# A decoder layer on one core: transposes handed out tile by tile, three jobs side by side at each stage entry, the last job by token tiles, and another beginning

## The chip, the core and the metric

The kernel runs on one core of one Trainium2 chip. The metric is the device time of one execution in microseconds; the median of several executions is taken. A difference is called faster or slower in the text below where it is over 0.2%.

## What is computed

One decoder layer for 256 tokens of width 2048, in float32, cut to its skeleton (16 heads of 128, inner width 5632 of the feed-forward nets; with 256 tokens the block-sparse attention is a plain causal one):

```
x = x + 0.5 * (silu(n(x) @ Wg1) * (n(x) @ Wu1)) @ Wd1        # FFN 1, n = RMSNorm with gain
z = n(x) @ W_in                                              # q, k, v, B, C, xt, two gates
y_a = attention(q, k, v) @ W_attn_out                        # causal, ALiBi
y_c = (B * causal_conv3(C * xt)) @ W_conv_out
x = x + (sigmoid(g_a) * y_a + sigmoid(g_c) * y_c) @ W_out
x = x + 0.5 * (silu(n(x) @ Wg2) * (n(x) @ Wu2)) @ Wd2        # FFN 2
out = n(x)
```

## The kernel before, in words

Weights are streamed once from memory, 467 MB in all, in chunks that are normally 128x1024 (512 KB). Each chunk passes three stages: a DMA issued by SP (`load`, L567) into one of five buffers; a cast on ACT to the matmul type, which gives the high part `hi` (L580); a subtraction on DVE, which gives the low part `lo` (L581). The weight is then used as hi + lo, and the activations are split in the same way (`split_col`: ACT L98 or L101, DVE L99 or L102). `hi` and `lo` have four buffers each. `parts` in the main loop cuts chunk n+4 into hi and lo while TensorE works on chunk n, and issues the load of chunk n+7, so at most a few chunks are ahead. ACT, DVE, PE and SP each work through their own queue in the order in which the program was written.

There are two kinds of jobs. A plain job (`job`, L183 and L184) multiplies one 128-column strip of weights with all 16 column tiles of the activations `xn`; it takes two chunks and 16 pairs of matmuls (512 and 256 columns), and its result is turned into the next activation by a few ACT and DVE operations, the job's `post`. A wide job (`wide_job`, L222 to L224) makes 512 columns of the residual for both token tiles: eight chunks, twelve 512-column matmuls for each chunk. Four wide jobs (nb = 0 to 3) close FFN 1, the mixer and FFN 2. Behind each of them `residual` adds to `x` (DVE L246 or L248), squares it for the next norm (ACT L132), and `turn` transposes the 512 new columns on TensorE (8 transposes, L236) and splits them into `xn` (L101, L102). A stage entry (seam) is the stretch from these four wide jobs to the next stage's first jobs: f1 to mixer and mixer to FFN 2.

Posts wait in a list, `pending`. After each chunk of a job one entry of it is written into the program (`flush(1)`). A step without chunks, such as the preload of the Sqrt table ahead of wide job nb = 1, writes all of them at once (`flush()`). The norm of a stage needs the sum over the four wide jobs. It is held back: `norm_steps` puts the first half behind the first plain job and the row of scales (two matmuls, L162) behind the second.

At the beginning `first_block` runs four plain jobs side by side in groups of four column tiles, with chunks of 256 KB, while x arrives transposed as `xin` (xT, SP). The sum of squares for the first norm is made from `xin` by 16 squares on ACT (L118, L121), 14 additions on DVE (L122) and matmuls with `ones` (L144), ahead of the block's last four pairs. The token-major `x` is loaded later, in four pieces, by SP. At the end the final norm scales the 2048 columns of both token tiles (DVE L644, ACT L646), and SP writes them out in four pieces of 512 KB. `load_gain` loads the final gain into one buffer for each last wide job (L262, SP).

## Time and profile before

| | |
|---|---|
| median of 3 runs | 2536.82 us (2535.48 to 2537.56) |
| the profiled execution, its own time | 2535.27 us |
| its span, first to last instruction | 2533.5 us |
| PE busy | 2485.4 us, 98% |
| PE weight loads | 2148.9 us, 85% |
| DVE busy | 1557.4 us, 61% |
| ACT busy | 1175.2 us, 46% |
| mean granted TensorE clock | 0.992 |
| read from memory | 466.68 MB, 185 GB/s over the span |

Busy time is that of instructions at work. A PE that waits or runs at the lower of its two clocks (1.2 of 2.4 GHz, a granted clock of 0.50 in a row) loses time in a way that the share does not show alike: the wait is idle, the slow matmuls count as busy. Times in rows count from the start of the span.

### The profile page before, as it was taken

The page shows a single profiled execution, that of the slowest core. Times are in us where ns is not written, and L with a number is a line of the kernel's source. Part 1 is how long each engine was busy: PE and PEld are TensorE (multiplying, and loading weights), DVE is VectorE, ACT ScalarE, POOL GpSimd, SP SyncE. Part 2 cuts the span into 40 slices and gives each one's busy share as a digit, 9 for nine tenths or more (in the row PEclk, how much of TensorE's full clock was granted, in tenths as well). Part 3 has the DMA queues.
Part 4 walks back from the last instruction along what each step waited for, and adds up shares of the span by engine and source line. Part 5 has one row for each costly group of instructions (what it writes and reads, how often), then busy time and mean ns, then how long its engine had stood idle before and what let it go on. Part 6 is the DMA issues. An engine that isn't in the chain of part 4 may idle for free.

```text
span 2533.5 us, 34394 instructions
## 1 busy us (share of the span) xinstructions
PE 2485.4 (98%) x13380; PEld 2148.9 (85%) x13380; DVE 1557.4 (61%) x2123; ACT 1175.2 (46%) x1685; POOL 1.9 (0%) x10
## 2 busy tenths in 40 slices
PE   8999999999999999999999999999999999999998
PEld 7888888888778888888888888887888888888886
DVE  6765665566546777655556666664566566556664
ACT  5544444344444444444444454444444444444443
POOL 0000000000000000000000000000000000000000
PEclk9999999999999999999999999999999999999999
DMA  7665556655555555555555545565556655665563
GB/s 242 204 194 192 190 186 197 192 191 185 174 151 181 191 190 184 192 192 190 189 168 180 170 167 191 190 184 146 172 189 192 190 191 192 191 192 191 191 198 143
DMA packets 131715, 471.02 MB, mean 186 GB/s; under 512 B 14560, under 2 KB 14688, under 8 KB 131552
## 3 DMA queue, kind: packets, MB, share of 16 engines
q1 hardware_dynamic: 131552, 468.84, 57.3%
q8 instruction: 104, 1.70, 0.3%
q14 instruction: 59, 0.48, 0.1%
HBM read 466.68 MB, written 2.10 MB: 185 GB/s over the span
## 4 chain that ended last, share of the span: by engine, by line
PE 96%; DVE 2%; ACT 1%; DMA 1%; issue 0%; SPq 0%; ACTq 0%; DVEq 0%
PE ps L183 46%; PE ps L184 23%; PE pv L222 7%; PE pv L224 7%; PE pv L223 7%; PE pv L447 1%; PE pv L445 1%; PE pv L446 1%; ACT hi L580 1%; DVE lo L581 1%; DVE xn L102 1%; DMA w<-in_wg 0%; ACT pv L132 0%; PE psV L502 0%; PE psS L468 0%
## 5 line engine op out<-in xcount | busy, mean ns | idle before, releaser
L183 PE MATMUL ps<-xn,hi 128*128 128x512 f32 x4544 | 1586.9, 393 | 0.0
L581 DVE TENSOR_TENSOR lo<-w,hi 128x1024 fp32r<-128x1024 f32 (+1 forms) x892 | 1076.1, 1211 | 810.8 <-ACT hi L580 809.9
L184 PE MATMUL ps<-xn,lo 128*128 128x256 f32 x4544 | 1271.6, 280 | 0.0
L580 ACT CAST hi<-w 128x1024 fp32r<-128x1024 f32 (+1 forms) x892 | 919.2, 1035 | 691.9 <-PE pv L224 272.2
L183 PEld LDWEIGHTS ps<-xn,hi 128*128 128x128 f32 x4544 | 854.9, 188 | 188.0
L184 PEld LDWEIGHTS ps<-xn,lo 128*128 128x128 f32 x4544 | 854.9, 188 | 0.7
L222 PE MATMUL pv<-hi,ring 128*128 128x512 f32 x832 | 327.1, 393 | 0.0
L223 PE MATMUL pv<-lo,ring 128*128 128x512 f32 x832 | 326.1, 392 | 0.0
L224 PE MATMUL pv<-hi,ring 128*128 128x512 f32 x832 | 326.0, 392 | 0.0
L224 PEld LDWEIGHTS pv<-hi,ring 128*128 128x128 f32 x832 | 157.6, 189 | 33.1
L223 PEld LDWEIGHTS pv<-lo,ring 128*128 128x128 f32 x832 | 157.8, 190 | 32.7
L222 PEld LDWEIGHTS pv<-hi,ring 128*128 128x128 f32 x832 | 157.8, 190 | 32.8
L197 DVE TENSOR_TENSOR t<-ps,c 128x256 f32<-128x256 f32 x320 | 134.0, 419 | 23.0 <-ACT c L195 23.0
L195 ACT COPY c<-ps 128x256 f32<-128x256 f32 x320 | 116.8, 365 | 54.4 <-PE ps L184 54.4
L98 ACT CAST ring<-hh 128x256 fp32r<-128x256 f32 x88 | 35.8, 406 | 201.1 <-DVE hh L321 201.1
L314 ACT ACTIVATE silu<-t 128x256 f32<-128x256 f32 x88 | 36.8, 418 | 163.1 <-DVE t L312 163.1
L183 PE MATMUL ps<-at,hi 128*128 128x512 f32 x256 | 89.5, 392 | 0.0
L183 PE MATMUL ps<-ring,hi 128*128 128x512 f32 x256 | 89.4, 392 | 0.0
L184 PE MATMUL ps<-ring,lo 128*128 128x256 f32 x256 | 71.6, 280 | 0.0
L184 PE MATMUL ps<-at,lo 128*128 128x256 f32 x256 | 71.6, 280 | 0.0
L99 DVE TENSOR_TENSOR ring<-hh,ring 128x256 fp32r<-128x256 f32 x88 | 37.5, 427 | 41.6 <-ACT ring L98 41.6
L183 PEld LDWEIGHTS ps<-ring,hi 128*128 128x128 f32 x256 | 48.1, 188 | 10.6
(102 smaller groups left out, 1013.8 us busy)
## 6 DMA issues: line engine op xcount, KB each, us to landing
w<-in_win SPq DMA_DIRECT2D x222, 512.0 KB, 4.1
w<-in_wd SPq DMA_DIRECT2D x176, 512.0 KB, 4.1
w<-in_wu SPq DMA_DIRECT2D x172, 512.0 KB, 3.9
w<-in_wg SPq DMA_DIRECT2D x170, 512.0 KB, 3.7
w<-in_wco SPq DMA_DIRECT2D x32, 512.0 KB, 3.6
w<-in_wv SPq DMA_DIRECT2D x32, 512.0 KB, 4.2
w<-in_wao SPq DMA_DIRECT2D x32, 512.0 KB, 3.9
w<-in_wo SPq DMA_DIRECT2D x32, 512.0 KB, 3.6
```

What stands on the lines that cost most here:

```text
L98: nc.scalar.copy(dst[:, 0:T], src)
L99: nc.vector.tensor_sub(dst[:, T:2 * T], src, f32(dst[:, 0:T]))
L183: nc.tensor.matmul(ps, hi[:, j * P:(j + 1) * P], r, start=(k == 0), stop=False)
L184: nc.tensor.matmul(ps[:, 0:T], lo[:, j * P:(j + 1) * P], r[:, 0:T], start=False, stop=(k == n - 1))
L195: nc.scalar.copy(c, ps[:, T:2 * T])
L197: nc.vector.tensor_add(t, ps[:, 0:T], c)
L222: nc.tensor.matmul(pv[i], xh, hi[:, cols], start=(k == 0), stop=False)
L223: nc.tensor.matmul(pv[i], xh, lo[:, cols], start=False, stop=False)
L224: nc.tensor.matmul(pv[i], xl, hi[:, cols], start=False, stop=(k == n - 1))
L314: nc.scalar.activation(s, g, AF.Silu)
L580: nc.scalar.copy(hi, w)
L581: nc.vector.tensor_sub(lo, w, f32(hi))
```

## The change

- `turn` works on one column tile (two transposes) where it worked on four, and `residual` returns the addition, an empty entry and four such turns, so that `flush(1)` hands them out behind six chunks of the next job.
- The first three jobs of the mixer and of FFN 2 run side by side (`side_block`) in groups of four column tiles, in twelve chunks of 256 KB; the norm's columns stand behind the sixth chunk, the row of scales behind the ninth. The four jobs at the beginning use the same function.
- The first norm is made from the token-major x (`row_square_in`, four squares for each token tile on ACT), which `fetch` now loads in the middle of the first block. The row of scales stands behind the fifth job, and the posts of the block are held back till then.
- x and xT are loaded by DMAs that ACT issues, the weights by SP. Six matmuls on zeros (f32, 256 columns) are put ahead of everything on TensorE.
- The last wide job is done as two jobs, one for each token tile, each with all eight weight chunks; behind the first one `finish(0)` scales token tile 0 and writes it out in three pieces, behind the second one `finish(1)` does tile 1 in four.

```diff
-X_LOAD = 24
+GK = 4
+WARM = 6
...
-    def add_square(tag, m):
...
+    def row_square_in(i):
+
+        if "f1" not in ssq:
+            ssq["f1"] = work.tile([P, 2, NB], F32, name="ssq", tag="ssq", bufs=2)
+        for nb in range(NB):
+            nc.scalar.activation(at[:, i, :], x[:, i, nb * NW:(nb + 1) * NW], AF.Square,
+                                 accum_out=ssq["f1"][:, i, nb:nb + 1])
...
+    def norm_cols(tag, i0=0, i1=2):
...
+        nc.vector.reduce_sum(s, ssq[tag][:, i0:i1, :], axis=AX.X)
...
-    def norm_steps(tag):
...
+    def rows(tag):
+        ps = norm_row(tag)
+        R[tag] = work.tile([P, T], F32, name="R", tag="R", bufs=1)
+        nc.vector.tensor_copy(R[tag], ps[:, 0:T])
...
-    def wide_job(chunks, src, post):
+    def wide_job(chunks, src, post, tiles=(0, 1)):
...
+            pv = {i: psum_big("pv") for i in tiles}
...
-                    for i in range(2):
+                    for i in tiles:
...
-    def turn(nb, gain):
-
-        for half, tag in ((0, "psT"), (1, "psV")):
-            ps = patt.tile([P, 4 * P], F32, name=tag, tag=tag)
-            for c in range(2):
-                m = nb * 4 + half * 2 + c
-                for i in range(2):
-                    nc.tensor.transpose(ps[:, c * T + i * P:c * T + (i + 1) * P], x[:, i, m * P:(m + 1) * P], ident)
-                split_col(xn[:, m, :], ps[:, c * T:(c + 1) * T], vec(gain, m))
+        return Step(chunks, pe, [lambda q=q: q(held[0]) for q in post], shift=0)
+
+    def turn(m, gain):
+
+        tag = ("psT", "psV")[m % 2]
+        ps = patt.tile([P, 4 * P], F32, name=tag, tag=tag)
+        for i in range(2):
+            nc.tensor.transpose(ps[:, i * P:(i + 1) * P], x[:, i, m * P:(m + 1) * P], ident)
+        split_col(xn[:, m, :], ps[:, 0:T], vec(gain, m))
 
...
                 if tag == "fin":
                     nc.vector.tensor_mul(yout[:, i, cols], x[:, i, cols], grow[nb])
+                    if nb == NB - 1:
+                        finish(i)
         if tag is None or tag == "fin":
             return [add]
-        return [add, lambda pv: turn(nb, gain)]
+        return [add, lambda _: None] + [lambda _, m=m: turn(m, gain) for m in range(4 * nb, 4 * nb + 4)]
+
+    def finish(i):
+
+        norm_cols("fin", i, i + 1)
+        r = rcol["fin"]
+        cuts = (0, 6, 11, 16) if i == 0 else (0, 4, 8, 12, 16)
+        for q, (a, b) in enumerate(zip(cuts, cuts[1:])):
+            cols = slice(a * P, b * P)
+            if q % 2 == 0:
+                nc.vector.tensor_scalar(yout[:, i, cols], yout[:, i, cols], r, None, op0=ALU.mult)
+            else:
+                nc.scalar.activation(yout[:, i, cols], yout[:, i, cols], AF.Copy, scale=r)
+            nc.sync.dma_start(out[:, i, cols], yout[:, i, cols])
 
...
-    def first_block(block, norms):
...
+    def side_block(block, rhs, hooks):
+
+        chunks = [(w[:, k * P:(k + GK) * P], GK) for k in range(0, ND, GK) for w, _ in block]
...
-                if b == 0 and k0 + GK < ND:
-                    prepare(k0 + GK, k0 + 2 * GK)
-                if b == 2:
-                    for k in range(k0, k0 + GK):
-                        add_square("f1", k)
-                if k0 + GK == ND and b == 2:
-                    norms[0].pe(None)
+                for h in hooks.get(n, ()):
+                    h()
                 yield
-            norms[1].pe(None)
-
-        return Step(chunks, pe, [lambda p=b[2], n=n: p(ps[n]) for n, b in enumerate(block)])
+
+        return Step(chunks, pe, [lambda p=b[1], n=n: p(ps[n]) for n, b in enumerate(block)])
+
+    def seam_hooks(tag):
+        return {5: [lambda: norm_cols(tag)], 8: [lambda: rows(tag)]}
 
...
+            for which, w, post in (("g", wg, post_g), ("u", wu, post_u)):
+                if len(block) < (4 if first else 3):
+                    block.append((w[t], post))
+                    if first and len(block) == 4:
+                        hooks = {n: [lambda k=n + 4: prepare(k, k + 4)] for n in (0, 4, 8)}
+                        hooks[1] = [lambda: fetch(0)]
+                        hooks[5] = [lambda: fetch(1)]
+                        hooks[12] = [lambda: row_square_in(0)]
+                        steps.append(Step([], lambda _: None, hold=True))
+                        steps.append(side_block(block, rhs, hooks))
+                    elif not first and len(block) == 3:
+                        steps.append(side_block(block, rhs, seam_hooks(tag)))
+                    continue
+                late = {}
+                if first and (which, t) == ("g", 2):
+                    late = {0: lambda: (row_square_in(1), norm_cols(tag)), 1: lambda: (rows(tag), release())}
+                steps.append(job((tag, which, t), pieces(w, t), rhs, post, late))
 
...
+                split_last = last and next_tag == "fin" and nb == NB - 1
+                for tiles in ((0,), (1,)) if split_last else ((0, 1),):
+                    steps.append(wide_job(wide(wd, nb, k0, k1), lambda k, k0=k0: ring((k0 + k) % RING),
+                                          residual(nb, 0.5, next_tag if last else None, gain_next), tiles))
...
+            if len(block) < 3:
+                block.append((win[part * ND + c], post))
+                if len(block) == 3:
+                    steps.append(side_block(block, rhs, seam_hooks("mix")))
+                return
...
-            q = len(raw) - X_LOAD
-            if q in (0, 2, 4, 6):
-                cols = slice(q * T, (q + 2) * T)
-                nc.sync.dma_start(x[:, :, cols], xt[:, :, cols])
...
+    def fetch(i):
+        nc.scalar.dma_start(x[:, i, :], xt[:, i, :])
+
     open_ring()
-    nc.scalar.preload_act_table(AF.Sqrt)
-    nc.sync.dma_start(xin[:, 0:2, :], xT[:, 0:2, :])
+    nc.scalar.dma_start(xin[:, 0:2, :], xT[:, 0:2, :])
     nc.sync.dma_start(cs[:, 0:NCST], cst)
     load(1)
-    nc.sync.dma_start(xin[:, 2:4, :], xT[:, 2:4, :])
-    load(2)
-    for i in range(1, 4):
-        nc.sync.dma_start(xin[:, 4 * i:4 * i + 4, :], xT[:, 4 * i:4 * i + 4, :])
-        load(min(LOAD_AHEAD, 2 + 2 * i))
-    nc.vector.memset(ones, 1.0)
+    nc.scalar.dma_start(xin[:, 2:4, :], xT[:, 2:4, :])
+    load(3)
+    nc.scalar.dma_start(xin[:, 4:8, :], xT[:, 4:8, :])
+    load(5)
+    nc.scalar.preload_act_table(AF.Sqrt)
+    nc.vector.memset(x[:, 0, 0:T], 0.0)
+    warm = patt.tile([P, 4 * P], F32, name="psS", tag="psS")
+    for _ in range(WARM):
+        nc.tensor.matmul(warm[:, 0:T], x[:, 0, 0:P], x[:, 0, 0:T], start=True, stop=True)
     make_identity(nc, ident)
...
+    nc.scalar.dma_start(xin[:, 8:12, :], xT[:, 8:12, :])
+    nc.scalar.dma_start(xin[:, 12:16, :], xT[:, 12:16, :])
...
-    norm_cols("fin")
-    r = rcol["fin"]
-    for q in range(2):
...
```

What this does to the order, at three places. First TensorE where the first wide job of the mixer's seam ends (pv: the wide jobs' accumulators, psT and psV: the two transpose buffers). Before:

```order
L224 MATMUL pv1_5980<-hi_6064,ring_91 128x512
L236 MATMUL psT_6139<-ident_85,x_79 128x128 x4
L236 MATMUL psV_6148<-ident_85,x_79 128x128 x4
L222 MATMUL pv0_6158<-hi_6082,ring_91 128x512
L223 MATMUL pv0_6158<-lo_6083,ring_91 128x512
```

and now, at the same place:

```order
L211 MATMUL pv_5943<-hi_6027,ring_90 128x512
L221 MATMUL psT_6102<-ident_84,x_79 128x128 x2
L221 MATMUL psV_6107<-ident_84,x_79 128x128 x2
L221 MATMUL psT_6112<-ident_84,x_79 128x128 x2
L221 MATMUL psV_6117<-ident_84,x_79 128x128 x2
L209 MATMUL pv_6123<-hi_6045,ring_90 128x512
```

The eight transposes of nb = 0 still stand in one clump ahead of the next wide job, in four pairs instead of two fours. Those of nb = 1, 2 and 3 stand apart, two behind each of four chunks of the following job.

Second DVE in the last wide job, where the split of tile 1's fourth chunk is over:

```order
L233 SCALAR_TENSOR_TENSOR x_79<-pv_22184,x_79 128x512
L238 TENSOR_TENSOR sacc_82<-x_79,grow_22182 128x512
L136 TENSOR_REDUCE rc_22303<-ssq_21873 128x1
L137 TENSOR_SCALAR rc_22303<-rc_22303 128x1
L139 RECIPROCAL rc_22303<-rc_22303 128x1
L140 TENSOR_TENSOR rc_22303<-rc_22303 128x1
L141 TENSOR_TENSOR rc_22303<-rc_22303 128x1
L142 TENSOR_SCALAR rc_22303<-rc_22303 128x1
L143 TENSOR_TENSOR rc_22303<-rc_22303 128x1
L253 TENSOR_SCALAR sacc_82<-sacc_82,rc_22303 128x768
L253 TENSOR_SCALAR sacc_82<-sacc_82,rc_22303 128x640
L579 TENSOR_TENSOR lo_22321<-w_22263,hi_22320 128x1024
```

All of tile 0's residual, norm and scaling now stands between the splits of two weight chunks, the last row being that of tile 1's fifth chunk; before, all this stood behind the last split.

Third SP at the same place (w_22318 is the last weight chunk of the program):

```order
L569 DMA w_22275<-in_wd2 128x1024
L569 DMA w_22288<-in_wd2 128x1024
L256 DMA out_y<-sacc_82 128x768
L256 DMA out_y<-sacc_82 128x640 x2
L569 DMA w_22318<-in_wd2 128x1024
L256 DMA out_y<-sacc_82 128x512 x4
```

The load of the last chunk has moved behind the three writes of tile 0; before, no write stood ahead of a load.

## Rows read from the trace of the kernel before

**Rows 1.** The profile's page: busy time of each engine

```profile
PE 2485.4 (98%) x13380; PEld 2148.9 (85%) x13380; DVE 1557.4 (61%) x2123; ACT 1175.2 (46%) x1685; POOL 1.9 (0%) x10
```

**Rows 2.** Who waited for whom, PE: total us, times, longest us

```profile
PE psT L236 <- DVE xn L102: 13.9, 8, 3.0
PE psV L236 <- DVE xn L102: 9.7, 8, 1.3
```

**Rows 3.** Windows: stretch, us, busy PE, PEld, DVE, ACT, POOL, clock, DMA share, GB/s

```profile
492.60:659.00 166.40, 166.40 (x961) 146.52 (x960) 108.32 (x148) 79.71 (x118) 0.00 (x0) 1.00 0.58 189
1250.00:1540.00 290.00, 290.00 (x1609) 253.14 (x1608) 180.21 (x280) 147.80 (x243) 0.00 (x0) 1.00 0.52 173
...
659.00:781.12 122.12, 109.77 (x487) 89.67 (x485) 59.41 (x74) 52.10 (x75) 0.00 (x0) 0.94 0.52 156
1682.48:1804.88 122.40, 110.06 (x486) 89.74 (x485) 59.83 (x74) 52.09 (x75) 0.00 (x0) 0.94 0.52 156
2180.89:2267.96 87.07, 87.07 (x386) 72.08 (x385) 44.81 (x43) 34.31 (x34) 0.00 (x0) 1.00 0.64 195
...
2521.43:2533.50 12.07, 0.16 (x1) 0.00 (x0) 4.76 (x13) 3.83 (x7) 0.00 (x0) 0.66 0.42 174
685.59:689.00 3.41, 3.41 (x10) 2.74 (x10) 0.66 (x2) 2.80 (x3) 0.00 (x0) 0.50 0.00 0
...
2527.00:2532.00 5.00, 0.00 (x0) 0.00 (x0) 0.00 (x0) 0.57 (x1) 0.00 (x0) 0.50 1.02 419
```

**Rows 4.** Timeline behind the mixer seam's first wide job: start, us, instruction, idle before

```profile
680.56 0.39 PE L224 MATMUL pv<-hi,ring 128*128 128x512 f32 x1
...
681.84 0.33 PE L236 MATMUL psT<-ident,x 128*128 128x128 f32 x1 [0.27 <-DVE x L248]
...
682.46 0.45 ACT L101 ACTIVATE xn<-psT,cs 128x256 fp32r<-128x256 f32 x1
682.94 0.48 DVE L102 SCALAR_TENSOR_TENSOR xn<-psT,cs,xn 128x256 fp32r<-128x256 f32 x1 [1.16 <-ACT xn L101]
683.48 0.44 PE L236 MATMUL psT<-ident,x 128*128 128x128 f32 x2 [1.32 <-DVE xn L102]
...
685.59 0.76 PE L222 MATMUL pv<-hi,ring 128*128 128x512 f32 x1
```

**Rows 5.** Timeline, PE, begin and end of the first block

```profile
5.60 0.79 PE L285 MATMUL ps<-xn,hi 128*128 128x512 f32 x1 [5.60 <-ACT hi L580]
...
35.56 1.87 PE L144 MATMUL psS<-ones,acc 128*128 128x1 f32 x8 [4.04 <-DVE acc L122]
...
40.60 0.48 PE L183 MATMUL ps<-xn,hi 128*128 128x512 f32 x1
```

**Rows 6.** Groups by form, 5 to 34 us: count, busy us, mean ns, idle before

```profile
L581 DVE TENSOR_TENSOR lo<-w,hi 128x512 fp32r<-128x512 f32 x16 | 10.5, 688 | 1.2 <-ACT hi L580 1.2
L580 ACT CAST hi<-w 128x512 fp32r<-128x512 f32 x16 | 9.6, 614 | 1.7 <-DMA w<-in_wg 1.1 <-PE ps L285 0.4
```

**Rows 7.** Groups by form, last wide job and tail (2499.66 us to the end)

```profile
L581 DVE TENSOR_TENSOR lo<-w,hi 128x1024 fp32r<-128x1024 f32 x5 | 6.0, 1223 | 5.0 <-ACT hi L580 4.8
...
L580 ACT CAST hi<-w 128x1024 fp32r<-128x1024 f32 x5 | 5.2, 1049 | 4.6 <-DMA w<-in_wd 2.7 <-PE pv L224 1.9
...
L248 DVE SCALAR_TENSOR_TENSOR x<-pv,x 128x512 f32<-128x512 f32 x4 | 2.7, 686 | 7.8 <-PE pv L224 7.8
L132 ACT ACTIVATE pv<-x 128x512 f32<-128x512 f32 x4 | 2.4, 603 | 12.9 <-DVE x L248 12.9
```

**Rows 8.** Timelines of SP, ACT and DVE, last wide job and tail

```profile
2504.87 0.33 SPq L262 DMA_DIRECT2D grow<-in_gf  x1
...
2509.47 1.05 ACT L580 CAST hi<-w 128x1024 fp32r<-128x1024 f32 x1 [2.71 <-DMA w<-in_wd]
...
2523.76 0.16 DVE L147 TENSOR_REDUCE rc<-ssq 128x2 f32<-128x8 f32 x1
...
2525.38 2.19 ACT L646 ACTIVATE sacc<-sacc,rc 128x1024 f32<-128x1024 f32 x2 [1.02 <-DVE rc L155]
```

More of the change, by code (lines that the diff above doesn't have):

```diff
@@ L83, in macaron_kernel @@
     cs = const.tile([P, NCST], F32, name="cs")
-    ones = const.tile([P, 4 * LINE], F32, name="ones")[:, 0:1]
     ident = const.tile([P, P], F32, name="ident")
     dist = const.tile([P, 3 * P], F32, name="dist")
-    work.tile([P, LINE], F32, name="padw", tag="padw", bufs=1)
+    work.tile([P, LINE + 120], F32, name="padw", tag="padw", bufs=1)
     def vec(off, i):
@@ L133, in row_square @@
                              accum_out=ssq[tag][:, i, nb:nb + 1])
-    def norm_cols(tag):
-        r = work.tile([P, 8], F32, name="rc", tag="rc", bufs=2)
-        v, s, y = r[:, 0:2], r[:, 2:4], r[:, 4:6]
-        if tag in acc:
-            ps = patt.tile([P, 4 * P], F32, name="psS", tag="psS")
-            a = acc.pop(tag)
-            for i in range(2):
-                for j, t in enumerate(a):
-                    nc.tensor.matmul(ps[:, i:i + 1], t[:, i * P:(i + 1) * P], ones, start=(j == 0), stop=(j == 1))
-            total = ps[:, 0:2]
-        else:
-            nc.vector.reduce_sum(s, ssq.pop(tag), axis=AX.X)
-            total = s
-        nc.vector.tensor_scalar(v, total, 1.0 / D, EPS, op0=ALU.mult, op1=ALU.add)
+    def row_square_in(i):
[5 more added lines that the diff above has]
+    def norm_cols(tag, i0=0, i1=2):
+        n = i1 - i0
+        r = work.tile([P, 8], F32, name="rc", tag="rc", bufs=3)
+        v, s, y = r[:, 0:n], r[:, 2:2 + n], r[:, 4:4 + n]
+        nc.vector.reduce_sum(s, ssq[tag][:, i0:i1, :], axis=AX.X)
+        nc.vector.tensor_scalar(v, s, 1.0 / D, EPS, op0=ALU.mult, op1=ALU.add)
         nc.scalar.activation(s, v, AF.Sqrt)
@@ L164, in norm_row, with job @@
         return ps
-    def norm_steps(tag):
-        def row(_):
-            ps = norm_row(tag)
-            R[tag] = work.tile([P, T], F32, name="R", tag="R", bufs=1)
-            nc.vector.tensor_copy(R[tag], ps[:, 0:T])
-        return (Step([], lambda _: norm_cols(tag), hold=True), Step([], row, hold=False))
-    def job(name, chunks, rhs, post):
+    def rows(tag):
+        ps = norm_row(tag)
+        R[tag] = work.tile([P, T], F32, name="R", tag="R", bufs=1)
+        nc.vector.tensor_copy(R[tag], ps[:, 0:T])
+    def job(name, chunks, rhs, post, hooks={}):
         n = sum(c[1] for c in chunks)
@@ L179, in pe @@
             k = 0
-            for hi, lo, nk in parts:
+            for n_done, (hi, lo, nk) in enumerate(parts):
                 for j in range(nk):
@@ L270, in switch @@
         steps.append(Step([], pe))
-    def first_block(block, norms):
-        GK = 4
-        chunks = [(w[t][:, k * P:(k + GK) * P], GK) for k in range(0, ND, GK) for w, t, _ in block]
+    def side_block(block, rhs, hooks):
+        chunks = [(w[:, k * P:(k + GK) * P], GK) for k in range(0, ND, GK) for w, _ in block]
         ps = []
@@ L324, in gu @@
             rhs = lambda k: xn[:, k, :]
-            if first and t < 2:
-                block.append((wg, t, post_g))
-                block.append((wu, t, post_u))
-                return
-            steps.append(job((tag, "g", t), pieces(wg, t, CK if t else CK // 2), rhs, post_g))
-            if t == 0:
-                steps.append(norms[0])
-            steps.append(job((tag, "u", t), pieces(wu, t), rhs, post_u))
-            if t == 0:
-                steps.append(norms[1])
+            for which, w, post in (("g", wg, post_g), ("u", wu, post_u)):
[15 more added lines that the diff above has]
+                steps.append(job((tag, which, t), pieces(w, t), rhs, post, late))
         t = 0
@@ L340, in ffn @@
                 t += 1
-                if first and t == 2:
-                    steps.append(first_block(block, norms))
             last = r == len(ROUNDS) - 1
@@ L361, in mixer @@
         held = {}
-        norms = norm_steps("mix")
+        block = []
         def win_job(part, c, post):
-            steps.append(job(("win", part, c), pieces(win, part * ND + c, CK // 2 if (part, c) == (4, 0) else CK),
-                             rhs, post))
+            if len(block) < 3:
[3 more added lines that the diff above has]
+                return
+            steps.append(job(("win", part, c), pieces(win, part * ND + c), rhs, post))
         for c in range(ND):
@@ L609, in macaron_kernel, with release @@
     pending = []
+    def release():
+        nonlocal holding
+        holding = False
     def flush(n=None):
```

41 lines of the change are left out of this document (9 added, 32 removed).

## The prediction

> **What bounds the kernel now.** I read the page first: TensorE is busy 98% of the span, and no other engine comes near [rows 1]. So only three things can pay: PE's idle time, time at its lower clock, and the head and tail of the program. The waits of PE come next. 23.6 us of idle time stand at the transposes L236, which wait for DVE's L102 [rows 2], and 4.0 us at the first norm's matmul [rows 5]. Then the windows, to see what the seams cost in all, since a slow matmul counts as busy. In undisturbed stretches a round of four wide jobs takes 87.07 us, so one of its 32 chunks takes 2.72 us, and 480 pairs of plain matmuls take 166.40 us, 0.347 us each [rows 3]. A seam, from the first wide job to the mixer's (or FFN 2's) third plain job, holds four wide jobs (87.07), 32 pairs (11.1), the scales' row (0.4) and 32 transposes. Two transposes take 0.44 us with a wait in it; I count 0.11 us for each, 3.5 us. That is 102.1 us, and the two seams last 122.12 and 122.40 us [rows 3]: 20.0 and 20.3 us are lost, more than the waits because PE comes out of some of them at the lower clock (685.59 to 689.00: clock 0.50, so 3.41 us of which half is lost) [rows 3].
>
> The timeline shows why. The transposes of the second token tile wait for DVE's addition until 681.84, ACT and DVE split that one column tile, and only when DVE has read it may PE write the same PSUM tile again, after 1.3 us of idle time [rows 4].
>
> **The seams.** The order shows two cases. For nb = 1, 2 and 3 two transposes stand behind each of four chunks. The addition is over long before the third chunk ends (2.3 us for ACT's and DVE's split of the chunk ahead, 2 x 0.69 for the additions: 3.7 us, against 8.2 us of three wide chunks [rows 7], or 4.2 us of three 256 KB chunks). Their ACT and DVE parts, about 0.46 and 0.48 us a tile [rows 4], fit beside a chunk's cast and subtraction (1.05 and 1.22 us [rows 7] in 2.72 us; 0.61 and 0.69 us [rows 6] in 1.39 us). If that cover went, the casts would fall behind PE, which is a rival below. I cost these turns at their 0.22 us on PE alone, which is in the 102.1.
>
> For nb = 0 the change does not do what it says: the Sqrt preload ahead of nb = 1 writes the whole list at once, so all eight transposes still wait for the addition. They alternate between two PSUM tiles, though. From rows 4: tile 0 is transposed at 681.84, split by ACT from 682.46 and by DVE to 683.42; tile 1 half a microsecond later, to 683.9; tiles 2 and 3 follow each at once, and the next wide job can begin at about 684.15 instead of 685.59. The last matmul before was issued at 680.56 and holds PE for 0.23 (87.07 us by 384), so from 680.79 on 3.35 us remain, 2.5 us beyond the transposes' own 0.87. Whether PE's clock falls there is open: 0 or 1.7 us, I take 0.85. What is left of a seam's loss is 3.35 us, and the gain 20.0 - 3.35 and 20.3 - 3.35, together **-33.6 us**. The bounds are -37 (all hidden but the addition) and -27 (the clock falls once or twice more in each seam).
>
> The norm now ends inside the side-by-side jobs: columns behind the sixth chunk need the sixth chunk's turn of DVE, 1.6 us (2523.76 to 2525.38 for the same steps [rows 8]), and the row's matmuls stand three chunks, 4.2 us, later. They wait for nothing.
>
> **The beginning.** Before, PE stood idle 4.04 us up to 35.56 for the first norm, spent 1.87 us on it, and then did the last four pairs and the row slowly until the fifth job began at 40.60 [rows 5]. Without the norm the block would have ended at 31.5 + 4 x 0.347 = 32.9. Two DMA queues and the dummy matmuls could move that: at best PE would run its 64 pairs without a gap from the first matmul at 5.60 [rows 5] on, 22.2 us, to 27.8. At worst the 2 MB of x, now fetched inside the block, take 2 MB / 419 GB/s [rows 3] = 5 us from the weights. ACT and DVE had hardly a wait for PE in that block (0.4 us of ACT's idle time at the casts [rows 6]) and more for DMA: a faster PE would wait for them. I take 32.5, nearly the row's own end. What the change puts in its place is the new wait: behind the block ACT has one cast (1.05), the four squares of tile 1 (each 0.60 and a read-out, 0.75), DVE the norm (1.6), ACT the next cast (1.05), DVE its subtraction (1.22), the copy of the row and the fifth accumulator's release (0.4 each). These stand in one chain, since the sixth job has no free PSUM buffer until the first post has read its own: 8.7 us, of which the cast partly overlaps the block's end; I take 8.2. PE's fifth job and the row need 6.0. So the sixth job starts at 32.5 + 8.2 = 40.7, where it was 40.60 + 16 x 0.347 = 46.15: **-5.4 us**, bounds -10 and 0.
>
> **The last job and the tail.** Twelve matmuls per chunk become six: a chunk lasts 1.36 us on PE and must be loaded, cast (1.05) and subtracted (1.22 us [rows 7]) in that time, 16 chunks instead of 8. PE itself needs 21.77 us, as before. Supply alone would just do: 524 KB in 1.36 us are 385 GB/s, and the rows show 419 GB/s of writes at a full share [rows 3], 20 us for 16 chunks, so 0 us. The Trainium skill (DMA: Bandwidth & Descriptors, section Specifications) gives about 358 GB/s as one core's limit on HBM; by that, an estimate, the 16 chunks take 23.4 us and the job would end at least 1.7 us late. No row here shows reads alone at a full share.
>
> What decides is the order. I count from the job's start (2499.66). DVE first ends the chunk split (2.3), then nb = 2's residual, two additions of 0.69 and two products as long [rows 7], to 5.1; the gain's load, which waits for it, was issued at 2504.87, 5.2 us in [rows 8], and the loads of chunks 6 and 7 stand behind it on SP. PE has eaten its four ready chunks at 5.4 and waits: chunk 4 is split at 7.4, 5 at 8.6. Chunk 6 lands at 2509.47, 9.8 in [rows 8], and is split at 12.1, chunk 7 at 13.3. Tile 0 ends at 14.5 instead of 10.9. Tile 1's four chunks then come one subtraction apart, the fourth at 18.4, done on PE at 19.9. Now `finish(0)` stands on DVE and ACT: addition 0.7, square 0.75 (0.60 [rows 7] and a read-out), norm 1.6, scaling of 1408 columns on DVE (at most 1.7 by the subtraction's row, I take 1.0) and 640 on ACT (0.7, from 2.19 for 2048 [rows 8]): DVE is free at 22.5, ACT at 22.2. Tile 1's fifth chunk is cast at 23.3 and split at 24.5: PE idles 4.6 us. The last load stands on SP behind three writes, the third of which needs DVE's last piece: issued at 23.2, behind 1 MB of writes (2.5 us at 419 GB/s [rows 3]), landed at about 27.2, cast 28.3, split 29.5. Six matmuls end it at 30.6, or 32.4 if the clock fell in the gap; I take 31.5: **+9.7 us** against 21.77, bounds +5 (writes and posts overlap better) and +12.
>
> The tail was 12.07 us [rows 3]: 3.95 us up to the scaling (2525.38 [rows 8]) and 8.1 us for scaling and 2 MB of writes. Now one tile is left: half of the writes (2.5 us at 419 GB/s) are out before, the residual has one tile less in its chain (about 0.7), and the first piece to be scaled is half as long (about 0.5): 8.4 us, **-3.7 us**. Together +6.0.
>
> **Sum.** -33.6 - 5.4 + 9.7 - 3.7 = -33.0 us on the profiled execution's 2535.27, so 2502.3. The median of the runs was 1.5 us above that execution; I forecast **2503.8 us**.
>
> **Rivals.**
> 1. *The last job keeps pace*: tile 0's finish slips between the splits without a gap, the last load is early. Then the term of 9.7 us is gone: 2494.1. For it: PE itself has no more work, and five raw and four split buffers hide much in the steady state. Against it: the order on DVE and SP. 12%.
> 2. *The spread turns wait after all*: ACT's queue is in order, so its half of a turn waits for PE's transposes and the next cast stands behind it; if the 256 KB chunks' short lead does not carry that, half of the seams' gain goes, 17 us: 2520.8. Against it: the cast is three chunks ahead (4.2 us), the wait at most one. 10%.
> 3. *The transposes keep the clock down* (slower than before). The 24 spread turns break into PE's stream; if each caused a stretch like the 3.41 us at 0.50 [rows 3], 1.7 us would be lost 24 times: +41 us, so 2544.8. It decides from 1.4 us a turn on (33.0 / 24). Against it: in the attention stage 16 heads' transposes stand between matmuls, three at a time, and the window keeps its clock at 1.00 and PE never idles [rows 3]. The Trainium skill (TensorE: Matmul & The Clock Gate, Part 4: PE-mode transpose) says that the full clock doesn't engage for transposes; by that rule, taken strictly, this rival would hold; the window speaks against it. 3%.
>
> **How the numbers follow.** The forecast has 72%, other mishaps 3%. Its bounds: the seams' -37 to -27, the beginning's -10 to 0, the last job's +1 to +8 with the tail; not all fall on one side, so its own range is 2495 to 2513. To hold 8 in 10 I go to rival 1 below and stop short of rival 2: 2493 to 2514. A measurement of this kernel tells 0.2%, 5 us, from no change. Only rival 3 and half of the mishaps are not faster: faster 0.95, same 0.02, slower 0.03.
>
> **What would show it.** In the profile after: no wait at the transposes but at nb = 0 of each seam, some 3 us; a seam of 105 us; the sixth job at about 41 us with a wait of some 2 us on DVE; in the last job a wait on ACT's cast at the fifth chunk and one of 4 to 5 us around tile 0's finish, and the last cast waiting for its DMA; a tail of 8.4 us. The forecast is wrong if the spread turns show waits in the waits' list, if the last job takes under 25 us, or if the first block ends before 29 or after 36.

## The result and the profile after

The changed kernel takes **2508.57 us** (median; 2507.59 to 2510.48), the kernel before 2536.51 beside it: ratio 0.9891, 95% interval 0.9874 to 0.9908. The forecast was 2503.8 us, its range 2493 to 2514. The profiled execution took 2509.3 us (before 2535.27) with a span of 2507.5. On the page TensorE, at 98% [rows 1], is now at 99%; no other engine comes near:

```profile
PE 2481.8 (99%) x13384; PEld 2143.0 (85%) x13384; DVE 1563.5 (62%) x2135; ACT 1183.8 (47%) x1703; POOL 1.9 (0%) x10
HBM read 470.88 MB, written 2.10 MB: 189 GB/s over the span
```

The waits of PE, changed kernel (waiting line, what it waited for: us, times, longest):

```profile
PE pv L209 <- ACT hi L578: 3.8, 4, 1.8
PE pv L210 <- DVE lo L579: 3.0, 4, 0.8
PE psT L150 <- DVE rc L143: 2.6, 1, 2.6
PE psT L221 <- DVE xn L102: 2.2, 2, 1.1
...
PE ps L169 <- DVE t L184: 1.2, 1, 1.2
```

The 23.6 us at the transposes [rows 2] have come down to 2.2 (and 1.2 on the additions, L231 and L233). New are 6.8 us at L209 and L210, the matmuls of the last job, where nothing stood before. The windows, in this order: the first seam, the low clock inside it, the second seam, the low clock after the beginning, the last job, the tail.

```profile
core 0: us, PE busy (x) PEld busy (x) DVE busy (x) ACT busy (x) POOL busy (x), PEclk, DMA share, GB/s
658.90:771.22 112.32, 110.67 (x519) 91.60 (x518) 61.67 (x80) 53.90 (x80) 0.00 (x0) 0.98 0.57 169
683.99:687.41 3.42, 3.42 (x10) 2.75 (x9) 1.17 (x3) 3.15 (x4) 0.00 (x0) 0.50 0.01 4
1666.78:1777.47 110.69, 109.03 (x519) 90.38 (x518) 61.88 (x80) 53.41 (x80) 0.00 (x0) 1.00 0.56 172
42.29:49.11 6.82, 5.67 (x17) 4.85 (x18) 4.26 (x9) 3.06 (x6) 0.00 (x0) 0.50 0.48 159
2466.46:2499.10 32.64, 25.76 (x97) 18.69 (x95) 21.71 (x28) 16.31 (x21) 0.00 (x0) 0.95 0.55 201
2499.10:2507.52 8.42, 0.00 (x0) 0.00 (x0) 3.37 (x11) 2.26 (x5) 0.00 (x0) 0.75 0.32 125
```

A seam is taken here from the first wide job's first matmul to the end of the third plain job's last one. The same stretch of before is 127.9 and 128.2 us; that is the 122.12 and 122.40 of [rows 3] plus one job and the last matmul's own end. The last round of before is taken to its last matmul's end too, so 0.16 us stand in it and not in the tail. So the 26 us between the two spans (2533.5 and 2507.5) split like this:

| part | before | after | measured | forecast |
|---|---|---|---|---|
| up to the first wide job | 162.72 | 162.61 | -0.1 | -5.4 |
| two seams | 127.9 + 128.2 | 112.3 + 110.7 | -33.1 | -33.6 |
| last round of four wide jobs | 87.23 | 97.94 | +10.7 | +9.7 |
| tail | 11.86 | 8.42 | -3.4 | -3.7 |
| all between | | | 0 | 0 |

Three of four terms came within 1.0 us of the forecast. The beginning did not.

One execution of the experiment e9 below took 8044.69 us at a mean granted clock of 0.30; its median there is that of the other three.

### The profile page after: what moved, and what is told of

Its sections match the earlier page's. It is cut to its first block, busy times and chain, and to the rows that moved or that the text cites. A ratio compares the mean times of both kernels' runs of the same rounds, so it can differ in the third digit from the quotient of the medians.

```text
span 2507.5 us, 34474 instructions
## 1 busy us (share of the span) xinstructions
PE 2481.8 (99%) x13384; PEld 2143.0 (85%) x13384; DVE 1563.5 (62%) x2135; ACT 1183.8 (47%) x1703; POOL 1.9 (0%) x10
## 4 chain that ended last, share of the span: by engine, by line
PE 97%; DMA 1%; DVE 1%; ACT 1%; issue 0%; SPq 0%; ACTq 0%
PE ps L169 45%; PE ps L170 23%; PE pv L211 7%; PE pv L210 7%; PE pv L209 7%; PE pv L449 1%; PE pv L447 1%; PE pv L448 1%; PE ps L284 1%; DMA w<-in_wu 1%; DMA w<-in_wd 1%; PE ps L285 1%; ACT hi L578 0%; DVE lo L579 0%; PE psV L504 0%; PE psS L470 0%
## 5 line engine op out<-in xcount | busy, mean ns | idle before, releaser
L169 PE MATMUL ps<-xn,hi 128*128 128x512 f32 x4448 | 1552.2, 393 | 1.2 <-DVE t L184 1.2
L170 PE MATMUL ps<-xn,lo 128*128 128x256 f32 x4448 | 1244.5, 280 | 0.0
L169 PEld LDWEIGHTS ps<-xn,hi 128*128 128x128 f32 x4448 | 836.2, 188 | 185.4 <-issue 1.3
L170 PEld LDWEIGHTS ps<-xn,lo 128*128 128x128 f32 x4448 | 836.3, 188 | 1.0 <-DVE lo L579 0.3
L209 PE MATMUL pv<-hi,ring 128*128 128x512 f32 x832 | 327.4, 393 | 3.8 <-ACT hi L578 3.8
L210 PE MATMUL pv<-lo,ring 128*128 128x512 f32 x832 | 325.6, 391 | 3.0 <-DVE lo L579 3.0
L209 PEld LDWEIGHTS pv<-hi,ring 128*128 128x128 f32 x832 | 156.9, 189 | 37.5 <-ACT hi L578 5.5
L210 PEld LDWEIGHTS pv<-lo,ring 128*128 128x128 f32 x832 | 157.2, 189 | 36.3 <-DVE lo L579 4.3
L211 PEld LDWEIGHTS pv<-hi,ring 128*128 128x128 f32 x832 | 157.1, 189 | 32.7
L182 ACT COPY c<-ps 128x256 f32<-128x256 f32 x320 | 116.7, 365 | 54.4 <-PE ps L170 54.4
L284 PE MATMUL ps<-xn,hi 128*128 128x512 f32 x160 | 58.0, 401 | 0.7 <-ACT hi L578 0.7
```

The lines of the kernel that those rows point to most:

```text
L169: nc.tensor.matmul(ps, hi[:, j * P:(j + 1) * P], r, start=(k == 0), stop=False)
L170: nc.tensor.matmul(ps[:, 0:T], lo[:, j * P:(j + 1) * P], r[:, 0:T], start=False, stop=(k == n - 1))
L182: nc.scalar.copy(c, ps[:, T:2 * T])
L209: nc.tensor.matmul(pv[i], xh, hi[:, cols], start=(k == 0), stop=False)
L210: nc.tensor.matmul(pv[i], xh, lo[:, cols], start=False, stop=False)
L211: nc.tensor.matmul(pv[i], xl, hi[:, cols], start=False, stop=(k == n - 1))
```

## The experiments

Theory at the start: the beginning's gain went into a new wait and the low clock behind it; what the seams still lose is the clump at nb = 0; the last job loses by the order of its work. Rivals stand in the texts. Edits are shown abridged. Stage times are read from each profile by the first and last matmul; "changed" is the kernel with the change.

| kernel | time, us | ratio to before [95%] | first wide job at | seams | last round | tail |
|---|---|---|---|---|---|---|
| changed | 2508.57 | 0.9891 [0.9874, 0.9908] | 162.61 | 112.3, 110.7 | 97.94 | 8.42 |
| e1 | 2502.31 | 0.9869 [0.9854, 0.9884] | 160.03 | 112.3, 112.1 | 87.23 | 12.02 |
| e2 | 2507.23 | 0.9888 [0.9874, 0.9903] | 161.09 | 112.3, 112.1 | 96.88 | 8.41 |
| e3 | 2497.50 | 0.9851 [0.9836, 0.9865] | 163.46 | 112.1, 110.7 | 87.23 | 8.41 |
| e4 | 2503.02 | 0.9872 [0.9855, 0.9888] | 162.51 | 108.5, 108.5 | 97.48 | 8.41 |
| e5 | 2509.18 | 0.9889 [0.9872, 0.9905] | 163.07 | 112.1, 110.7 | 97.77 | 8.41 |
| e6 | 2508.90 | 0.9890 [0.9875, 0.9905] | 161.47 | 110.7, 112.3 | 98.68 | 8.53 |
| e7 | 2491.11 | 0.9821 [0.9806, 0.9835] | 160.64 | 108.3, 108.3 | 87.23 | 8.53 |
| e8 | 2504.19 | 0.9878 [0.9864, 0.9891] | 157.01 | 112.3, 110.7 | 98.14 | 8.53 |
| e9 | 2503.98 | 0.9875 [0.9859, 0.9890] | 157.14 | 110.7, 112.4 | 98.67 | 8.54 |
| e11 | 2508.97 | 0.9894 [0.9881, 0.9908] | 161.51 | 110.7, 112.1 | 98.28 | 8.41 |
| e10 | 2486.73 | 0.9807 [0.9793, 0.9820] | 156.81 | 108.5, 108.5 | 87.23 | 8.53 |
| e12 | 2488.28 | 0.9814 [0.9801, 0.9827] | 158.18 | 108.5, 108.5 | 87.23 | 8.54 |

Everything between the stages is the same in all to 0.02 us (496.3, 895.6 and 623.7 us), so a stage that an edit leaves alone shows the scatter of one execution: 160.03 to 163.46 for the beginning, which is the same code in the changed kernel and e1 to e4.

### The last job

**e1**: the last job and the end as before.

```
-split_last = last and next_tag == "fin" and nb == NB - 1
+split_last = False
...
+norm_cols("fin")
...
```

> The last job is done as before the change (both tiles in one job, each weight chunk loaded and split once, norm and scaling after it); the rest is the changed kernel. Theory: the last job by token tiles costs 10.6 us in the job (32.3 us in the trace of the changed kernel against 21.8) and gives back 3.4 us in the tail (8.7 against 12.1), so this kernel is 7.2 us faster than the changed one: span 2500.3 us, last job 21.8 us, tail 12.1 us. Rival: the waits in the last job only move elsewhere and the shorter tail is what counts: the span then grows by 3.4 us, to 2510.9.

Measured: 87.23 and 12.02, so -10.7 in the round and +3.6 in the tail: -7.1 us, as expected. (The rest of the span's -8.3 is the beginning's scatter and a seam's.) The last job's part of the change costs 7 us net; the rival falls.

**e2**: tile 0's finish later.

```
-if nb == NB - 1:
+if nb == NB - 1 and i == 1:
     finish(i)
...
+if tag == "fin" and nb == NB - 1:
+    return [add, lambda _: None, lambda _: None, lambda pv: finish(0) if 0 in pv else None]
```

> Tile 0's norm, scaling and writes are issued only after the last chunk's split and load; tile 0's addition and square stay where they are. Theory (order): the waits from 2489.3 us on in the trace of the changed kernel (1.8, 0.8, 0.55, 0.8 us, 3.9 us in all) vanish, and the last cast no longer waits 3.0 us for its DMA; the waits before (0.6, 0.8, 0.9, 0.8) stay. Last job about 28.4 us, time 3 to 4 us below the changed kernel, tail no longer than 9.5 us. Rival (supply): twice as many chunks, 16 of 512 KB, are too much for the loads or the splits; the job stays at 31 to 32 us and the time does not change by more than 1 us.

Measured: the round takes 1.1 us less, not 3 to 4, and the last job 31.6 us, as the rival (supply) has it. The edit did less than its text says: in the trace the finish still stands ahead of one cast, the last.

```profile
2485.61 0.60 ACT L120 ACTIVATE pv<-x 128x512 f32<-128x512 f32 x1 [1.89 <-DVE x L233]
2487.32 0.49 PE L209 MATMUL pv<-hi,ring 128*128 128x512 f32 x1 [0.47 <-ACT hi L580]
2488.58 0.50 PE L210 MATMUL pv<-lo,ring 128*128 128x512 f32 x1 [0.77 <-DVE lo L581]
2492.29 0.83 ACT L257 ACTIVATE sacc<-sacc,rc 128x640 f32<-128x640 f32 x1 [1.00 <-DVE rc L143]
2493.03 1.03 ACT L580 CAST hi<-w 128x1024 fp32r<-128x1024 f32 x1
2494.11 0.51 PE L209 MATMUL pv<-hi,ring 128*128 128x512 f32 x1 [1.37 <-ACT hi L580]
```

The last load is no longer late, but PE waits where the addition and square of tile 0 (2485.6) stand among the splits, and again behind the finish. Order alone, then, is not all: a chunk lasts 1.36 us on PE and its subtraction 1.23 on DVE, so a lead that DVE loses to 2 us of other work hardly comes back. Nor do the loads leave room. In the changed kernel, behind the gain's load:

```profile
2473.00:2483.00 10.00, 7.55 (x24) 5.46 (x24) 7.29 (x7) 5.79 (x6) 0.00 (x0) 0.83 0.98 356
```

The DMA share is 0.98 at 356 GB/s (0.99 at 371 in e2's trace), so 512 KB take 1.4 to 1.5 us where PE needs 1.36. How much of the 10.7 us is the order and how much the doubled chunk rate stays open; the next run takes both away.

**e3**: end by token tiles, but split each chunk once (`apart` is 4 in the last job, None elsewhere; `post[0]` is tile 0's residual and finish).

```
+if apart is not None and c >= apart:
+    kept.append((hi, lo, 2 * c))
+    columns(hi, lo, 2 * c, tiles[:1])
 else:
     columns(hi, lo, 2 * c, tiles)
 yield
+if kept:
+    post[0]({0: pv[0]})
+    for hi, lo, k in kept:
+        columns(hi, lo, k, tiles[1:])
```

> Each weight chunk of the last job is loaded and split once: chunks 0 to 3 for both token tiles as before the change, then chunks 4 to 7 for tile 0 alone, tile 0's finish, and chunks 4 to 7 (kept in the four split buffers) for tile 1. Theory: what hurt the last job is that chunks come twice as fast and stand behind tile 0's finish; here neither holds, so the job takes 21.8 to 23 us, and the tail stays at about 8.7 us since tile 0's finish and writes lie beside the last 5.4 us of TensorE: 9 to 10.5 us below the changed kernel. Rival: to end by token tiles is what costs, because tile 0's finish (about 6 us of VectorE) holds up tile 1's addition: tail 11 us or more, gain 7 us or less.

Measured: windows of the last job and of the tail,

```profile
2467.10:2489.07 21.97, 21.97 (x97) 17.85 (x96) 12.19 (x20) 8.26 (x13) 0.00 (x0) 1.00 0.21 76
2489.07:2497.49 8.42, 0.01 (x1) 0.00 (x0) 3.37 (x11) 2.26 (x5) 0.00 (x0) 0.76 0.54 209
```

PE is busy for all 21.97 us, and the tail is as short as with the change: -10.7 us and nothing given back; the time falls by 11 us. What hurt was not to end by tiles but to load and split each chunk twice for it, with what that put in DVE's and SP's queues. The rival, a tail of 11 us or more, falls.

### The seams

**e4**: the Sqrt preload ahead of nb = 1 no longer flushes the list (FFN 1 and mixer).

```
-steps.append(Step([], lambda _: nc.scalar.preload_act_table(AF.Sqrt)))
+steps.append(Step([], lambda _: nc.scalar.preload_act_table(AF.Sqrt),
+                  hold=None if next_tag == "fin" else False))
...
-steps.append(Step([], lambda _: nc.scalar.preload_act_table(AF.Sqrt)))
+steps.append(Step([], lambda _: nc.scalar.preload_act_table(AF.Sqrt), hold=False))
```

> The Sqrt preload ahead of the second wide job no longer writes the list of pending work at once (in both seams), so the transposes of nb = 0 are given out two at a time like the others. Theory: of what the two seams still lose (4.6 and 3.0 us over 107.5) the clump at nb = 0 is nearly all: the waits at its transposes and the stretch of 3.41 us at clock 0.50 behind it vanish, the seams take 108 us each, and the time falls by 6 to 7.5 us. Rival: what is lost lies in the block of three jobs and its norm, or the turns wait one by one instead: the time falls by less than 2 us.

```profile
658.81:767.31 108.50, 108.50 (x519) 90.33 (x518) 61.75 (x80) 52.51 (x79) 0.00 (x0) 1.00 0.58 176
1662.87:1771.41 108.54, 108.54 (x519) 90.32 (x518) 62.57 (x81) 53.67 (x81) 0.00 (x0) 1.00 0.58 176
```

Measured: seams shorter by 3.8 and 2.2 us, the time by 5.5 (expected 6 to 7.5), PE busy in every microsecond of them, clock 1.00; against 107.8 (the prediction's 102.1, a job and 0.16) 0.7 us is left in each. So the clump at nb = 0 was nearly all that the seams still lost, and 32 transposes given out two at a time neither wait nor lower the clock. The Trainium skill (TensorE: Matmul & The Clock Gate, Part 4: PE-mode transpose) says that the full clock doesn't engage for transposes; among matmuls it stays, by these two windows.

### The beginning

**e5**: no dummy matmuls (`WARM = 0`).

> The dummy matmuls of the beginning are left out (two DMA queues and all else stay). Theory: the first block is held by loads, ScalarE and VectorE and not by TensorE's clock, so it ends within 1 us of 32.95 us (the changed kernel's) although TensorE runs its first pairs at the low clock, and the time is within 1.5 us of the changed kernel's. Rival: the early full clock is what the new beginning gains, the block ends 2 to 4 us later and the time grows by as much.

Measured: the full clock is granted from 11.41 us on instead of 4.74, the first block ends at 35.02 (the same beginning with dummies: 32.05 to 34.71 in five traces; the changed kernel's is 33.12 by the last matmul's end), the first wide job starts inside the scatter, and the time is unchanged. The block's end was expected within 1 us of the changed kernel's; it is 1.9 us later and 0.3 above the highest of the five. What the dummies give in the time can't be told from nothing.

**e6**: squares spread, norm earlier.

```
-hooks[12] = [lambda: row_square_in(0)]
+for n, i, n0, n1 in ((7,0,0,2), (9,0,2,3), (10,0,3,4), (12,1,0,1), (13,1,1,2), (14,1,2,4)):
+    hooks.setdefault(n, []).append(lambda i=i, n0=n0, n1=n1: row_square_in(i, n0, n1))
+hooks[14].append(lambda: norm_cols(tag))
...
-late = {0: lambda: (row_square_in(1), norm_cols(tag)), 1: lambda: (rows(tag), release())}
+late, ck = {2: lambda: (rows(tag), release())}, CK // 2
```

> The squares of x are spread over the first block (tile 0 behind its chunks 7, 9 and 10, tile 1 behind 12, 13 and 14) instead of four at its end and four behind it, the norm's columns stand behind chunk 14, and the fifth job's chunks are halved so that the row stands behind its third. Theory: what ate the beginning's 5.4 us is the chain squares, norm, row, first post, PSUM buffer, and the low clock that its waits of 2.6 and 1.2 us leave for 6.83 us; with the chain ended 3 us sooner the sixth job starts at 39 us instead of 43.4 at the full clock, the first wide job starts at 155.5 to 157 us instead of 162.6, and the time falls by 5.5 to 7 us. Rival: the 2 MB of x in that block take loads from the weights, and the beginning is bound by them however the chain lies: the block ends later or the casts wait for DMA, and the gain is 2 us or less.

Measured: the wait for the norm is gone and so is the low clock, yet the first wide job starts at 161.47 and the time is the same. My theory had fallen. New waits of PE stand at 59 to 67 us, 1.7 us in all, and ScalarE's timeline ahead of them shows why (L182 is the copy with which a post begins):

```profile
46.32 0.41 ACT L98 CAST ring<-hh 128x256 fp32r<-128x256 f32 x1 [2.27 <-DVE hh L316]
46.63 1.04 ACT L581 CAST hi<-w 128x1024 fp32r<-128x1024 f32 x1
47.58 0.36 ACT L182 COPY c<-ps 128x256 f32<-128x256 f32 x1
49.82 0.42 ACT L309 ACTIVATE silu<-t 128x256 f32<-128x256 f32 x1 [1.88 <-DVE t L307]
50.14 1.03 ACT L581 CAST hi<-w 128x1024 fp32r<-128x1024 f32 x1
51.08 0.37 ACT L182 COPY c<-ps 128x256 f32<-128x256 f32 x1
```

Four posts have piled up behind the scales' row and go out one per chunk. Each holds ACT 1.9 to 2.3 us for DVE, with the next cast behind it: 7.4 us for two chunks (43.68 to 51.08 from copy to copy), while PE needs 5.56. In all nine traces so far the first wide job starts 119.9 to 121.7 us after the first of these copies, wherever the sixth job began. That alone proves nothing: in the kernel before and in the changed kernel PE doesn't wait for a post's chunk there.

**e8**: e6, and the rest of a post (Silu, or split into the ring) behind the next cast: `rest` is issued at the start of the next flush.

```
-nc.scalar.activation(s, g, AF.Silu)
+rests.append(rest)
...
-split_col(ring(t % RING), hh)
+rests.append(lambda: split_col(ring(t % RING), hh))
```

> The start of the sixth kernel of this study (squares spread over the first block) and one thing more: what follows a post's last product (the Silu, or the split into the ring) is issued behind the next chunk's cast instead of before it. New theory, from the traces so far: the first posts wait together for the scales' row and are then worked off one per chunk, each holding ScalarE's queue up so that one takes 3.7 us and a chunk on TensorE 2.8, so the first wide job starts 120 to 121.7 us after the first post's copy, wherever the sixth job began. With the cast ahead the copies come 2.8 us apart, no wait of TensorE is left between 45 and 162 us, and the first wide job starts at 158 to 159.5 us instead of 161.5: 2 to 3.5 us. Rival (loads): the pace of 3.7 us comes from late weights or TensorE itself; the copies stay 3.7 us apart and nothing changes.

Measured: copies at 41.31, 43.49, 45.83, 48.14, so 2.3 us apart, the cast (L585) now ahead of the wait for DVE, which is shorter:

```profile
43.49 0.37 ACT L182 COPY c<-ps 128x256 f32<-128x256 f32 x1
43.76 1.05 ACT L585 CAST hi<-w 128x1024 fp32r<-128x1024 f32 x1
45.50 0.42 ACT L312 ACTIVATE silu<-t 128x256 f32<-128x256 f32 x1 [0.70 <-DVE t L308]
```

PE's one wait after the first block is 0.9 us for the PSUM buffer; the first wide job at 157.01, 4.5 us earlier than in e6 and 3.0 below the lowest of the five traces with the beginning of the change. Of the 4.5 us, 1.6 lie ahead of the sixth job (40.45 against 42.07) and 2.8 behind it, where e6 had its three waits: with the norm early, the pace of the posts was the bound. The time falls by 4.4 us, just under the 0.2% that count here as faster.

**e9**: e8, and `psV` as the sixth job's accumulator.

```
-ps = psum_big("ps")
+ps = patt.tile([P, 2 * T], F32, name="psV", tag="psV") if own else psum_big("ps")
```

> As the one before, and the sixth job takes a PSUM tile of its own (psV, which nothing uses so early) instead of the first accumulator's. Theory: the sixth job then waits for no post; from the end of the first block to the first wide job nothing but TensorE's own 122.5 us is left (352 pairs of 0.347 us and the row), so that job starts at 156 to 157.5 us, and the time is 4 to 6 us below the changed kernel's. Rival (loads): with the wait gone TensorE runs into casts that wait for weights behind the 2 MB of x, and gains 1 us or less over the one before.

From the first block's end to the first wide job, the changed kernel and this one:

```profile
33.12:162.61 129.49, 125.66 (x709) 109.99 (x709) 86.37 (x129) 66.07 (x106) 0.00 (x0) 0.97 0.59 192
```
```profile
34.83:157.14 122.31, 122.31 (x709) 107.71 (x708) 85.37 (x129) 64.47 (x99) 0.00 (x0) 1.00 0.64 208
```

PE is busy throughout, in 122.31 us, 7.2 less than with the change. Since this trace's first block ended late (34.83; 33.50 in e8), the first wide job and the time are those of e8; what the edit gives over e8, 1.2 us of the stretch, does not show there.

**e11**: the rests alone, in the changed kernel.

> The changed kernel with the one edit that the rest of a post is issued behind the next chunk's cast; squares, norm and PSUM tiles as changed. Theory: the copies come 2.8 us apart instead of 3.7, the sixth job still waits for the norm and starts at 42 to 43.5 us, and with the pace gone the first wide job starts 116.6 us later plus what the low clock takes (0, 1.7 or 3.4 us): 158.8 to 163 us; the time changes by 2 us at most. Rival: the pace of the posts is all there was, the first wide job starts before 158 us and the time falls by 4 us or more.

Measured: copies 2.8 us apart from 49.15 us on, the sixth job still late (43.4) with a stretch of 3.41 us at clock 0.50 behind it, the first wide job at 161.51, the time unchanged. Neither edit pays alone: behind the late norm and the low clock the posts' pace costs PE nothing, and with the norm early it costs what that gained.

### Together

**e7** is e3, e4 and e6; **e10** is e3, e4 and e9.

> The last three edits that theory expects to pay in one kernel: the last job apart by tiles from chunk 4 on, the transposes of nb = 0 spread too, the squares of x spread over the first block. They lie in different stages, so theory adds them: 9.5 + 7 + 6.5 = 23 us below the changed kernel, about 2485.5 us. Rival: one of them costs elsewhere what it gives (loads or casts displaced into the next stage): 2490 us or more.

> The last job apart by tiles from chunk 4 on, the transposes of nb = 0 spread too, and the beginning of the kernel before the last (squares spread, rest of a post behind the next cast, a PSUM tile of its own for the sixth job). Theory: 10.3 (last job) + 5.8 (seams) + 5 (beginning) = 21 us below the changed kernel, 2486 to 2488.5 us, and 3 to 5 us below the one with the three first edits. Rival: the beginning stays where the loads let it, and the time stays at 2490 to 2491 us.

Measured: 2491.11 and 2486.73 us. In e7 the beginning gives 2 us and not 6.5, as e6 by itself gave about 1; the rest adds up. So the time is the rival's, over 2490 us, but not for its reason: no edit costs elsewhere what it gives. e10 is 22 us below the changed kernel and 4.4 below e7, as expected.

**e12**: e10 with the loads of x behind chunks 8 and 12; the squares follow in the fifth job, the scales' row in the sixth.

```
-hooks[1] = [lambda: fetch(0)]
-hooks[5] = [lambda: fetch(1)]
+hooks[8].append(lambda: fetch(0))
+hooks[12] = [lambda: fetch(1)]
```

> The kernel with all edits (the one at 2486.7 us), with the two 1 MB loads of x issued behind chunks 8 and 12 of the first block instead of 1 and 5; the squares follow in the fifth job and the scales' row in the sixth, where the first accumulator is free in time. Loads theory: the first block still takes 28.0 us from 6.5 to 34.5, 5.8 more than its 64 pairs need, because x's 2 MB stand among its weights (ScalarE's casts wait 9.1 us for DMA up to 60 us); without them the block ends at 31 to 33 us, the first wide job starts 122.5 us later, at 153.5 to 155.5 us instead of 156.8, and the time falls by 1.5 to 3 us. Rival: the loads of the weights and of x transposed alone hold the block, or ScalarE and VectorE do: it ends at 33.5 to 35 us and the time does not change, or the casts behind the block now wait for x in their turn and the gain is given back.

Measured: the first block ends 2.1 us earlier (32.43), as the loads theory has it, but then the casts wait, and PE with them, and after that PE waits for the later norm:

```profile
37.44 1.05 ACT L598 CAST hi<-w 128x1024 fp32r<-128x1024 f32 x1 [2.22 <-DMA w<-in_wu]
38.54 0.49 PE L169 MATMUL psV<-xn,hi 128*128 128x512 f32 x1 [0.56 <-ACT hi L598]
39.80 0.38 PE L170 MATMUL psV<-xn,lo 128*128 128x256 f32 x1 [0.77 <-DVE lo L599]
43.95 0.68 PE L150 MATMUL psT<-ident,rc 128*128 128x128 f32 x4 [1.32 <-DVE rc L143]
```

The first wide job starts 1.4 us later than in e10, and the time is 1.5 us more, the same within 0.2%. So the gain is given back, as the rival has it: half in waits for a chunk's cast and subtraction (0.56 and 0.77 us), half in the wait for the norm (1.3), whose squares had to follow the loads. Whether another place for the 2 MB would cost less stays open.

## Why the prediction was right, and where it failed

**The seams**: right, -33.1 against -33.6. The reading that the preload's flush leaves nb = 0 clumped is what the trace shows:

```profile
681.74 0.33 PE L221 MATMUL psT<-ident,x 128*128 128x128 f32 x1 [0.27 <-DVE x L233]
681.90 0.38 PE L221 MATMUL psV<-ident,x 128*128 128x128 f32 x2
683.39 0.44 PE L221 MATMUL psT<-ident,x 128*128 128x128 f32 x2 [1.10 <-DVE xn L102]
683.78 0.53 PE L221 MATMUL psV<-ident,x 128*128 128x128 f32 x2
683.97 0.77 PE L209 MATMUL pv<-hi,ring 128*128 128x512 f32 x1
```

The next wide job starts at 683.97 (forecast 684.15, in the time of before; before 685.59 [rows 4]). I took half a stretch of low clock for each seam; the first had one (1.7 us), the second none, so that the mean was met by luck. Rivals 2 and 3 are out: no spread turn waits or lowers the clock. Rival 1 falls with the next term.

**The last job and the tail**: right in place and nearly in size, +10.7 and -3.4 against +9.7 and -3.7. Four places, as forecast:

```profile
2471.66 0.33 SPq L262 DMA_DIRECT2D grow<-in_gf  x1
2476.53 1.04 ACT L578 CAST hi<-w 128x1024 fp32r<-128x1024 f32 x1 [2.99 <-DMA w<-in_wd]
2489.39 2.92 ACT L578 CAST hi<-w 128x1024 fp32r<-128x1024 f32 x3
2490.66 0.69 SPq L569 DMA_DIRECT2D w<-in_wd  x1
2495.32 1.05 ACT L578 CAST hi<-w 128x1024 fp32r<-128x1024 f32 x1 [3.00 <-DMA w<-in_wd]
```

The gain's load at 5.2 us into the job, chunk 6, loaded behind it, cast at 10.1 (forecast: landed at 9.8), the casts resumed after the finish at 22.9 (forecast: the fifth chunk of tile 1 cast at 23.3, so begun at 22.2), the last load issued at 24.2 (forecast 23.2), its cast begun at 28.9 (forecast 27.2). Each of the last three is 0.7 to 1.7 us late; the term's error is 1.0. Not all in it was as forecast. PE's wait around the finish was shorter than the 4.6 us forecast for it (1.78 and 0.76 us, and 0.55 and 0.77 at the last chunk), but a stretch of 3.41 us at clock 0.50 stands ahead of it. And supply, put at 0 us by the 419 GB/s of writes, ran at 356 to 371 GB/s in reads (see e2), less than the 385 that PE's pace asks for; what that cost by itself stays open.

**The beginning**: wrong, -0.1 against -5.4 (between +0.7 and -2.7 in the five traces with this beginning), and with it most of the miss: 7.0 us on the profiled execution, 2509.3 against 2502.3. On the medians it is 4.8 us, since the median lies 0.7 below the profiled execution and not, as forecast, 1.5 above; that is luck. The range held because it is 21 us wide, not because this term was right. The first block gave way to the fifth job at 32.95 (forecast 32.5). The step that failed is "so the sixth job starts at 32.5 + 8.2 = 40.7", taken as if the gain there were the gain at the end. The rows:

```profile
32.77 1.05 ACT L578 CAST hi<-w 128x1024 fp32r<-128x1024 f32 x1 [0.70 <-DMA w<-in_wg]
34.57 1.05 ACT L578 CAST hi<-w 128x1024 fp32r<-128x1024 f32 x1 [0.76 <-DMA w<-in_wu]
35.87 1.05 ACT L578 CAST hi<-w 128x1024 fp32r<-128x1024 f32 x1 [0.24 <-DMA w<-in_wu]
36.82 0.63 ACT L128 ACTIVATE at<-x 128x512 fp32r<-128x512 f32 x1
39.84 0.16 DVE L136 TENSOR_REDUCE rc<-ssq 128x2 f32<-128x8 f32 x1 [1.66 <-ACT at L128]
40.34 1.03 ACT L578 CAST hi<-w 128x1024 fp32r<-128x1024 f32 x1
41.28 0.36 ACT L182 COPY c<-ps 128x256 f32<-128x256 f32 x1
41.57 0.68 PE L150 MATMUL psT<-ident,rc 128*128 128x128 f32 x4 [2.61 <-DVE rc L143]
43.44 0.77 PE L169 MATMUL ps<-xn,hi 128*128 128x512 f32 x1 [1.19 <-DVE t L184]
```

First, the chain took 10.5 us instead of 8.2 (from 32.95 to 43.44): tile 1's squares begin at 36.82, behind three casts and 1.7 us of their waits for DMA, where I had set one cast. Second, I costed nothing behind the sixth job. PE came out of these waits at clock 0.50 for 6.83 us (window 42.29 to 49.11, 17 matmuls), which ate the 2.7 us that were left. Six traces show what lies behind the sixth job (us):

| kernel | sixth job at | first wide job at | between | in it |
|---|---|---|---|---|
| before | 46.24 | 162.72 | 116.5 | nothing |
| changed | 43.44 | 162.61 | 119.2 | clock 0.50 up to 49.11 |
| e1 | 42.27 | 160.03 | 117.8 | one wait of 0.8 behind a post |
| e6 | 42.07 | 161.47 | 119.4 | three waits behind posts, 1.7 |
| e8 | 40.45 | 157.01 | 116.6 | nothing |
| e9 | 40.66 | 157.14 | 116.5 | nothing |

PE alone needs 116.5 us here. Where the clock did not fall, the posts' pace took 1.3 us (e1, and e2 alike), and 2.9 once the norm came earlier (e6). e8 and e9 show that no third cause is needed: with chain and pace mended the sixth job starts at the forecast's 40.7, nothing is lost behind it, and the 5.4 us are there (162.72 before, 157.0 and 157.1).

## What to carry to other kernels

A job that starts earlier can gain nothing where the work that was held back ahead of it is then released at a slower pace: follow the queue of held-up work until it is empty, not to the first job after the wait. In an engine's in-order queue put the feeder's instruction (here the next cast) ahead of one that waits for another engine. To end by halves, part the matmuls and keep the split weights; don't feed them twice.
